# Two moves in the second layer: heads' products in turns on the two column halves, and slots and gathers of units 1 and 2 ahead of the experts' order

## The chip, the core and the metric

One core of a Trainium2 chip runs the whole program in one launch. The metric is the device time of an execution in microseconds; lower is better. TensorE (PE in the profile), VectorE (DVE), ScalarE (ACT), GpSimd (POOL) and the DMA queue of SyncE (SP) each work through their own list of instructions in order.

## The reference

A backbone of two layers over 256 latent tokens and 256 context tokens of width 1024, all in float32. Only the second (odd) layer is touched by the change. Cut to what matters:

```python
# odd mixer, latent tokens only (last layer)
y = concat([pool_branch(u_pool), latent_attention(q, k, v, k_c, v_c, sink)]) @ w_out
h = h + m[2] * y
f = modulate(rmsnorm(h, norm_ffn_g), m[3], m[4])
# latent_attention, per block of 128 queries and head: 8 heads of 64, 2 key/value heads
p = softmax(concat([s_lat, s_ctx, sink]))       # 256 latent + 256 context keys
o = p_lat @ v + p_ctx @ v_ctx
# grouped_moe: 16 experts, top 2 of one group of 4
out = sum_e combine[:, e] * ((silu(f @ w_gate[e]) * (f @ w_up[e])) @ w_down[e])
h = rmsnorm(h + m[5] * out)
```

## The kernel before

Everything in the second layer works on two chunks of 128 tokens. A tile framework schedules the written program: it orders the instructions of each engine by a timing model of its own, so a change in one place moves instructions around it.

**Weights** come as tiles of 1 MB (128 x 2048 floats) from one stream in a fixed order (`Stream`, line 100). `load` (L134 on) issues a tile's DMA on SP as soon as one of 13 places is free; `take`, `half` and `done` hand them to the matrix products and free them. Experts that are alone in a unit have each tile split into a high and a low part first (`_prep`: ACT makes `whi` at L176, DVE or POOL makes `wlo` at L180), and a product is then three products (`mm3`, L516, whose records are L517 to L519). An odd_w_out tile is treated the same way. Modulation weights (`ada`, L445) are multiplied as they are, in four strips of 32 columns of TensorE.

**Attention.** Eight units (`units`: a block of 128 queries b, a pair of heads c). `scores(b, c)` makes both heads' scores (L1498), the softmax on DVE and ACT (L1502 to L1518) and leaves `p` with 2 x 512 probabilities per query. `attend(b, c)` transposes p of one head in four pieces (L1530), copies them to `pTT` (L1532; DVE for the first head, ACT for the second) and multiplies the values by it in four products that add up (L1535). The first head's products write partitions 0 to 63 of the bank, the second's 64 to 127, so each uses one half of TensorE's columns. Between the units stand the pool branch (L1478, L1484), modulation weights (L445) and products with odd_w_out (`mix`).

**Experts.** The 16 experts stand in units of one (S), two (P) or four (Q): "PPSPSPPQ". A unit with n experts gives each 128/n of 128 slots. The first five experts, thus units 0, 1 and 2, are fixed; the others are put in order of load by `order` (from L984), whose result also chooses which expert's weights SP loads from there on (`ids`, a load into a register at L301). `arrange` (L1010) turns the token ranks into that order. `slots1(n)` finds with DVE compares (L1646) and TensorE products (L1650) which token sits in each slot; `gather1(n)` fetches these rows by an indirect DMA from POOL (L1664); `xpose1(n)` transposes them (L1679). For unit 0 `xpose1` gets the tokens by products with the slot matrix (L1682) and needs no gather. The loop over units then takes the up product, hidden, the transposition of the next unit, and its gate product (`gu`, records L933), with the down products (`down1`, L967) of the unit before. The gathered tile `xg` shares its two buffers with `f0` and `f1`, the layer's normed tokens, and `sgm` has two buffers.

Of the kernel before, what the change touches and what calls it, by code (L numbers as in the profile page):

```python
# [10 lines left out]
F32 = mybir.dt.float32  # L11
# [15 lines left out]
FIXED = (2, 5)  # L27
# [185 lines left out]
def backbone(ctx: ExitStack, tc: tile.TileContext, I, out):  # L213
    nc = tc.nc
    V, S, G, T, Q = nc.vector, nc.scalar, nc.gpsimd, nc.tensor, nc.sync
# [14 lines left out]
    def y_t():  # L230
        return psum.tile([128, 512], F32, name="yp", tag="yp", bufs=2)

    def tr_t():
        return psum.tile([128, 512], F32, name="tr", tag="tr", bufs=2)
# [107 lines left out]
    for half in range(2):  # L342
        v = owo[512:1024, half * 512:half * 512 + 512].rearrange("(j c d) n -> j d c n", j=2, c=4)
# [177 lines left out]
    def split(hi, lo, x, eng):  # L521
        i = S.activation(hi, x, AF.Copy)  # L522
        eng.tensor_sub(lo, x, hi.bitcast(F32))  # L523
        return i
# [117 lines left out]
    with phase("even") as ep:  # L642
# [78 lines left out]
        def banks4():  # L721
            return [mm_t() for _ in range(4)]
# [22 lines left out]
        b = banks4()  # L745
# [5 lines left out]
        b = banks4()  # L751
# [6 lines left out]
        b = banks4()  # L758
# [7 lines left out]
        b = banks4()  # L766
# [114 lines left out]
        for half in range(2):  # L881
            banks = [mm_t() for _ in range(4)]
            hs = slice(half * 512, half * 512 + 512)
# [102 lines left out]
    def order(l, pool, nch, oh):  # L986

        pk = tr_t()
        for c in range(nch):
            T.matmul(pk[0:16, 0:16], one[:, 0:16], oh[:, c], start=(c == 0), stop=(c == nch - 1))  # L990
        t16 = lambda n, name: pool.tile([16, n], F32, name=name, tag=name)
        key, kd, kc, place, over, cap = t16(16, "key"), t16(16, "kd"), t16(1, "kc"), t16(1, "place"), t16(1, "over"), t16(1, "cap")
        V.scalar_tensor_tensor(key, pk[0:16, 0:16], 32.0, kb[l], op0=OP.mult, op1=OP.add)
        V.tensor_mul(kd, key, idt[0:16, 0:16])
        V.tensor_reduce(kc, kd, axis=AX.X, op=OP.add)
        V.tensor_scalar(kd, key, kc, None, op0=OP.is_ge)
        V.tensor_reduce(place, kd, axis=AX.X, op=OP.add)
        perm = t16(16, "perm")
        V.tensor_scalar(perm, ior[0:16, 0:16], place, None, op0=OP.is_equal)
        pt = tr_t()  # L1000
        T.matmul(pt[0:1, 0:16], eid[0:16], perm, start=True, stop=True)
        V.tensor_copy(ids[l], pt[0:1, 0:16])
        V.tensor_mul(kd, perm, caps[l])
        V.tensor_reduce(cap, kd, axis=AX.X, op=OP.add)
        V.tensor_scalar(over, kc, kbe[l], 1.0 / 32, op0=OP.subtract, op1=OP.mult)
        V.tensor_sub(over, over, cap)
        return perm, cap, over
# [126 lines left out]
    with phase("moe0") as mp:  # L1134
# [17 lines left out]
        def id_weights(name, cw, n):  # L1152

            t = mp.tile([128, 4, n, 4], F32R, name=name)
            for j in (0, 3):
                V.tensor_copy(t[:, :, :, j], idk[:, :, None].to_broadcast([128, 4, n]))
            V.tensor_copy(t[:, :, :, 1], cw[:, :, 0:n])
            V.tensor_sub(t[:, :, :, 2], cw[:, :, 0:n], t[:, :, :, 1].bitcast(F32))
            return t

        ranks, idw = pm, id_weights("idw2", comb, 2)
        units = UNITS[0]
# [166 lines left out]
        for c in range(2):  # L1329
            t = ("whi", "wlo")[c]  # L1330
# [19 lines left out]
    with phase("odd") as op:  # L1350
# [14 lines left out]
        vv = op.tile([128, 4, 128], F32, name="vv")  # L1365
# [91 lines left out]
        for b in range(2):  # L1457
            pt = tr_t()
# [6 lines left out]
        pt = tr_t()  # L1465
# [55 lines left out]
        ob = {}  # L1521

        def attend(b, c):
            p = PN.pop((b, c))
            if c == 0:
                ob[b] = y_t()
            for v in range(2):
                pt = tr_t()
                for q in range(4):
                    T.transpose(pt[:, q * 128:(q + 1) * 128], p[:, v, q * 128:(q + 1) * 128], idt)  # L1530
                pT = op.tile([128, 4, 128], F32, name="pTT", tag="pTT", bufs=2)
                (S.copy if v else V.tensor_copy)(pT.rearrange("p k t -> p (k t)"), pt)  # L1532
                hs = slice(v * 64, v * 64 + 64)
                for q in range(4):
                    T.matmul(ob[b][hs, c * 128:(c + 1) * 128], vv[:, q, hs], pT[:, q], start=(q == 0), stop=(q == 3),  # L1535
                             skip_group_check=True)
            if c == 3:
                bs = slice(b * 128, b * 128 + 128)
                split(mT[1][0][:, :, bs], mT[1][1][:, :, bs], ob[b].rearrange("p (c t) -> p c t", c=4), V)

        units = [(b, c) for b in range(2) for c in range(4)]
# [32 lines left out]
        for n, u in enumerate(units):  # L1574
            if n + 1 < len(units):
                scores(*units[n + 1])
            if n < 4:
                f = pool_group(n)
            attend(*u)
            if n < 4:  # L1580
                f()
            if n < 6 - NPRE:
                ada(*next(ada_it))
            if n == 4:
                flush()
                rows(1, 3, 5, 1)
                t = op.tile([128, 2, D], F32, name="s4b", tag="band")
# [32 lines left out]
    with phase("moe1") as mp:  # L1620
# [5 lines left out]
        units = UNITS[1]  # L1626
# [12 lines left out]
        def slots1(n):  # L1639

            u = units[n]
            w = 128 // len(u)
            sg = mp.tile([128, 2, 128], F32, name="sgm", tag="sgm", bufs=2)
            for c in range(2):
                for h, p in enumerate(u):
                    V.tensor_scalar(sg[:, c, h * w:h * w + w], ior[:, 0:w], ranks[:, c, p:p + 1], None, op0=OP.is_equal)  # L1646
            pw_ = tr_t()
            m = 2 * len(u)
            for c in range(2):
                T.matmul(pw_[:, 0:m], sg[:, c], idw[:, c, u[0]:u[0] + len(u)].rearrange("p e j -> p (e j)"),  # L1650
                         start=(c == 0), stop=(c == 1))
            for h in range(len(u)):
                hs = slice(h * w, h * w + w)
                V.tensor_scalar(sli[hs, n:n + 1], pw_[hs, 2 * h + 1:2 * h + 2], OFF, None, op0=OP.add)
            t = mp.tile([128, 1], F32, name="slw1", tag="slw1", bufs=4)
            for h in range(len(u)):
                hs = slice(h * w, h * w + w)
                V.tensor_copy(t[hs], pw_[hs, 2 * h:2 * h + 1])
            slw[n] = t
            return sg  # L1660

        def gather1(n):
            xg[n] = cp.tile([128, D], F32, name=f"xg{n}", tag="H1", bufs=2)
            return G.indirect_dma_start(out=xg[n], out_offset=None, in_=fd1,  # L1664
                                        in_offset=bass.IndirectOffsetOnAxis(ap=sli[:, n:n + 1], axis=0),
                                        bounds_check=255, oob_is_err=False)

        def xpose1(n, sg=None):

            xh = mp.tile([128, KD, 128], F32R, name="xh1", tag="xh", bufs=2)  # L1670
            xl = mp.tile([128, KD, 128], F32R, name="xl1", tag="xl", bufs=1) if len(units[n]) == 1 else None
            for hf in range(2):
                pt = tr_t()
                for q in range(4):

                    ks = slice(hf * 4 + q, D, 8)
                    o = pt[:, q * 128:(q + 1) * 128]
                    if sg is None:
                        T.transpose(o, xg[n][:, ks], idt)  # L1679
                    else:  # L1680
                        for c in range(2):
                            T.matmul(o, f1[c][:, ks], sg[:, c], start=(c == 0), stop=(c == 1))  # L1682
                fs = slice(hf * 4, hf * 4 + 4)
                if xl is None:
                    (V.tensor_copy if hf else S.copy)(xh[:, fs].bitcast(F32).rearrange("p k t -> p (k t)"), pt)
                else:
                    split(xh[:, fs], xl[:, fs], pt.rearrange("p (k t) -> p k t", k=4), V)
            xT[n] = (xh, xl)
# [23 lines left out]
        st.more(1, lambda: Two(x_t("wa", "X"), x_t("wb", "X")))  # L1712
        st.load()
        idw = id_weights(comb)
        xpose1(0, slots1(0))
        perm, cap, over = order(1, mp, 2, oh)
        st.limit = st.upto = 1 << 30
        st.load()
# [1 line left out]
        pg = gu("g", 1, 0, *xT[0])  # L1720
        ranks, combS, ranksT = arrange(1, mp, 2, perm, pm, comb, "amt")
        idw = id_weights(combS)
        for n in (1, 2):
            slots1(n)
            gather1(n)
        reg = any_over(mp, over)
# [29 lines left out]
        for half in range(2):  # L1756
            hs = slice(half * 512, half * 512 + 512)
# [107 lines left out]
```

## Time and profile before

| | |
|---|---|
| median of 3 runs (lowest, highest) | 1009.97 us (1009.04, 1010.44) |
| the profiled execution's own time | 1012.91 us |
| its span, first to last instruction | 1011.1 us |
| mean granted TensorE clock | 0.958 of full |
| busy: PE, DVE, ACT, POOL | 92%, 53%, 34%, 34% |
| DMA moved | 296.28 MB, mean 293 GB/s |

An fp32 product leaves two records on PE, a transposition one: "x8" at L1535 is four products. PE's busy time is modelled and neighbours overlap by some 0.07 us, so the length of a group is best read from its start to the next group's start. A bracket at a row's end tells how long the engine stood idle before it, and for what.

### The profile page before, as it was taken

To read this page: it belongs to the slowest core of one execution; us is meant where nothing else is said; L and a number is where in the kernel's file an instruction comes from. 1 tells how busy PE (TensorE), PEld (TensorE's weight loads), DVE (VectorE), ACT (ScalarE), POOL (GpSimd) and SP (SyncE) were. 2 spreads that over 40 slices of the span, in tenths; PEclk is the share of its full clock that TensorE was granted. 3 is DMA by queue.
4 is the path that set the end of the run, shared out by engine and by line. 5 is a ranking of instruction groups with operands and counts; after the bars stand their busy time and mean duration, and the time that the engine had idled before them with its cause. 6 is when DMAs were issued, how large, how long until landed. Compare 5 with 4: busy or idle time off the path is not lost. (4 is left out here: it accounts for less than half of the span.)

```text
span 1011.1 us, 12687 instructions
## 1 busy us (share of the span) xinstructions
PE 927.9 (92%) x4662; PEld 583.7 (58%) x4662; DVE 532.2 (53%) x921; ACT 340.3 (34%) x488; POOL 346.5 (34%) x239
## 2 busy tenths in 40 slices
PE   4999999978899999999999788999976999999973
PEld 2677677746675678558746567457553355544321
DVE  4552525286783777457935774547443265643212
ACT  4322113144563266246534362333211132411001
POOL 3350103335562746525823633023000143452112
PEclk9999999998899999999999989799977999999988
DMA  9973668948699799799699872296568799999993
GB/s 316 363 266 125 230 252 290 352 167 299 214 321 374 245 344 362 264 340 387 219 363 385 292 237 84 94 308 237 191 232 326 293 418 407 370 384 419 420 397 132
DMA packets 116276, 296.28 MB, mean 293 GB/s; under 512 B 6632, under 2 KB 16888, under 8 KB 105704
## 3 DMA queue, kind: packets, MB, share of 16 engines
q1 hardware_dynamic: 110184, 278.06, 75.0%
q0 software_dynamic: 5984, 17.26, 4.7%
q8 instruction: 40, 0.66, 0.3%
q14 instruction: 36, 0.29, 0.1%
q10 hardware_dynamic: 32, 0.01, 0.0%
HBM read 295.45 MB, written 4.24 MB: 296 GB/s over the span
## 5 line engine op out<-in xcount | busy, mean ns | idle before, releaser
L176 ACT ACTIVATE whi<-w 128x1024 fp32r<-128x1024 f32 x182 | 190.7, 1058 | 221.9 <-PE mm L519 87.0
L180 POOL TENSOR_TENSOR wlo<-w,whi 128x1024 fp32r<-128x1024 f32 x64 | 164.6, 2572 | 258.8 <-ACT whi L176 206.0
L180 DVE TENSOR_TENSOR wlo<-w,whi 128x1024 fp32r<-128x1024 f32 x118 | 181.1, 1546 | 92.5 <-ACT whi L176 91.8
L933 PE MATMUL mm<-w,xh 128*64 128x512 f32 (+1 forms) x616 | 150.9, 617 | 4.8 <-DMA w<-in_moe_w_up_dram 4.8
L528 POOL TENSOR_TENSOR H<-H,am 128x512 f32<-128x512 f32 x64 | 89.7, 1420 | 125.3 <-DVE am L527 122.9
L933 PEld LDWEIGHTS mm<-w,xh 128*64 128x64 f32 (+1 forms) x616 | 43.8, 135 | 88.4 <-issue 78.1
L517 PE MATMUL mm<-whi,xh 128*128 128x512 f32 x192 | 79.3, 413 | 1.9 <-DVE am L527 1.1
L518 PE MATMUL mm<-wlo,xh 128*128 128x512 f32 x192 | 78.6, 409 | 2.7 <-DVE wlo L180 2.3
L519 PE MATMUL mm<-whi,xl 128*128 128x512 f32 x192 | 78.1, 407 | 0.0
L527 DVE TENSOR_TENSOR am<-mm,m5b 128x512 f32<-128x512 f32 x64 | 42.9, 684 | 28.7 <-PE mm L1261 19.5
L1261 PE MATMUL mm<-y,seT 128*128 128x512 f32 x208 | 54.5, 397 | 0.2 <-ACT y L522 0.2
L517 PE MATMUL mm<-aTh,whi 128*128 128x512 f32 x128 | 52.4, 415 | 1.0 <-ACT aTh L678 1.0
L518 PE MATMUL mm<-aTl,whi 128*128 128x512 f32 x128 | 51.6, 403 | 1.1 <-POOL aTl L679 1.1
L519 PE MATMUL mm<-aTh,wlo 128*128 128x512 f32 x128 | 51.1, 400 | 0.0
L1261 PEld LDWEIGHTS mm<-y,seT 128*128 128x128 f32 x208 | 38.1, 188 | 15.5 <-issue 4.9
L518 PEld LDWEIGHTS mm<-wlo,xh 128*128 128x128 f32 x192 | 37.4, 195 | 14.4 <-DVE wlo L180 3.4
L517 PEld LDWEIGHTS mm<-whi,xh 128*128 128x128 f32 x192 | 37.5, 195 | 14.0 <-issue 4.2
L445 PE MATMUL yp<-w,sT 128*32 128x512 f32 x288 | 44.0, 624 | 0.0
L519 PEld LDWEIGHTS mm<-whi,xl 128*128 128x128 f32 x192 | 37.4, 195 | 7.7 <-DVE xl L523 0.3
L517 PE MATMUL yp<-whi,hh 128*128 128x512 f32 x96 | 38.2, 397 | 0.7 <-ACT hh L1067 0.7
L1053 DVE SCALAR_TENSOR_TENSOR sg<-sg,slw,mm 128x512 f32<-128x512 f32 x21 | 15.6, 742 | 43.9 <-PE mm L933 41.1
L518 PE MATMUL yp<-wlo,hh 128*128 128x512 f32 x96 | 38.4, 400 | 0.0
(363 smaller groups left out, 1545.2 us busy)
## 6 DMA issues: line engine op xcount, KB each, us to landing
w<-in_moe_w_gate_dram SPq DMA_DIRECT2D x60, 1024.0 KB, 11.3
w<-in_moe_w_down_dram SPq DMA_DIRECT2D x59, 1024.0 KB, 10.5
w<-in_moe_w_up_dram SPq DMA_DIRECT2D x57, 1024.0 KB, 9.7
w<-in_ada_w_dram SPq DMA_DIRECT2D x48, 1024.0 KB, 10.1
w<-in_even_w_in_dram SPq DMA_DIRECT2D x8, 1024.0 KB, 9.6
w<-in_odd_w_in_dram SPq DMA_DIRECT2D x5, 1024.0 KB, 14.3
w<-in_even_w_out_dram SPq DMA_DIRECT2D x4, 1024.0 KB, 7.9
s4b<-mrow SPq DMA_DIRECT2D x6, 512.0 KB
```

Source lines behind the costliest of these rows:

```text
L176: self.nc.scalar.activation(hi, t, AF.Copy)
L180: eng.tensor_sub(lo, t, hi.bitcast(F32))
L445: T.matmul(pa[32 * j:32 * j + 32, :], s_at(s * 4 + j, u), t[:, j, :], start=first and s == 0, stop=last and s == 1, skip_group_check=True)
L517: T.matmul(o, lh, rh, start=first, stop=False)
L518: T.matmul(o, lh, rl, start=False, stop=False)
L519: T.matmul(o, ll, rh, start=False, stop=last)
L527: V.tensor_mul(t, pp, m)
L528: eng.tensor_add(acc, acc, t)
L933: T.matmul(o[hs], xh[:, kk, hs].bitcast(F32), w[h][:, k], start=first and k == 0, stop=last and k == 3, skip_group_check=True)
L1053: V.scalar_tensor_tensor(sg, sg, w, pu, op0=OP.mult, op1=OP.mult)
L1261: marks["comb"] = T.matmul(pp, seT[n][:, c * 128:(c + 1) * 128], t[:, hs], start=(i == 0), stop=(i == 2 * len(ns) - 1))
```

## The change

In `attend`, both heads' pieces are now transposed and copied first, and the eight products then go in turns: piece 0 of the first head, piece 0 of the second, piece 1 of the first, and so on. In the experts' stage, `slots1(1)` now stands between `slots1(0)` and `xpose1(0)`, `gather1(1)` behind `xpose1(0)`, then `slots1(2)` and `gather1(2)`, all ahead of `order`; they use the ranks from before the sorting, which are the same for fixed experts. The same two calls behind `arrange` are gone. Lines behind the first edit are numbered three higher in the changed kernel, and those behind the second eleven higher.

```diff
             if c == 0:
                 ob[b] = y_t()
+            pT = []
             for v in range(2):
                 pt = tr_t()
                 for q in range(4):
                     T.transpose(pt[:, q * 128:(q + 1) * 128], p[:, v, q * 128:(q + 1) * 128], idt)
-                pT = op.tile([128, 4, 128], F32, name="pTT", tag="pTT", bufs=2)
-                (S.copy if v else V.tensor_copy)(pT.rearrange("p k t -> p (k t)"), pt)
-                hs = slice(v * 64, v * 64 + 64)
-                for q in range(4):
-                    T.matmul(ob[b][hs, c * 128:(c + 1) * 128], vv[:, q, hs], pT[:, q], start=(q == 0), stop=(q == 3),
+                pT.append(op.tile([128, 4, 128], F32, name="pTT", tag="pTT", bufs=2))
+                (S.copy if v else V.tensor_copy)(pT[v].rearrange("p k t -> p (k t)"), pt)
+
+            for q in range(4):
+                for v in range(2):
+                    hs = slice(v * 64, v * 64 + 64)
+                    T.matmul(ob[b][hs, c * 128:(c + 1) * 128], vv[:, q, hs], pT[v][:, q], start=(q == 0), stop=(q == 3),
                              skip_group_check=True)
...
         idw = id_weights(comb)
-        xpose1(0, slots1(0))
+
+        ahead = [n for n in (1, 2) if units[n][-1] < FIXED[1]]
+        sg0 = slots1(0)
+        slots1(1)
+        xpose1(0, sg0)
+        gather1(1)
+        for n in ahead[1:]:
+            slots1(n)
+            gather1(n)
         perm, cap, over = order(1, mp, 2, oh)
...
-        for n in (1, 2):
+        for n in range(1 + len(ahead), 3):
             slots1(n)
             gather1(n)
```

**PE, units 0 and 1 of attention.** (tr is a bank for transpositions, yp one for sums, sT the conditioning columns.) Before:

```order
L1530 MATMUL tr<-idt,p 128x128 x8
L1535 MATMUL yp<-pTT,vv 64x128 x4
L1484 MATMUL tr<-pT,pw 128x256
L445 MATMUL yp<-w,sT 32x512 x5
L1535 MATMUL yp<-pTT,vv 64x128 x4
L445 MATMUL yp<-w,sT 32x512 x3
L1478 MATMUL tr<-band,U 128x256 x2
L445 MATMUL yp<-w,sT 32x512 x5
L1530 MATMUL tr<-idt,p 128x128 x4
L445 MATMUL yp<-w,sT 32x512 x11
```

Now:

```order
L1531 MATMUL tr<-idt,p 128x128 x8
L1538 MATMUL yp<-pTT,vv 64x128
L1484 MATMUL tr<-pT,pw 128x256
L445 MATMUL yp<-w,sT 32x512 x9
L1538 MATMUL yp<-pTT,vv 64x128 x7
L1478 MATMUL tr<-band,U 128x256 x2
L1531 MATMUL tr<-idt,p 128x128 x4
L445 MATMUL yp<-w,sT 32x512 x15
L1498 MATMUL mm<-kT,qT 128x512 x2
```

The first product of a unit goes alone where the first four went, and the other seven stand where the second four stood. The modulation products (L445) between them stand in groups of 9 and 15 instead of 5, 3, 5 and 11. Over all eight units the L445 groups counted in products are 5, 3, 5, 11, 5, 1, 2 and 4, 1, 11 before, and 9, 15, 8 and 11, 5 now. The products of the last two units stand as one group of eight, those of the other six as one and seven. Scores (L1498) behind unit 0's products stand four times alone and twice as a pair before, twice alone and three times as a pair now.

**PE, from the end of unit 0's up products to the gate products of unit 1.** (xh is the transposed input, idw the slots' token numbers and weights.) Before:

```order
L933 MATMUL mm<-w,xh_6447 64x512 x11
L1019 MATMUL tr<-perm,pmT 128x16 x2
L1024 MATMUL tr<-idt,comb 16x128 x2
L1029 MATMUL tr<-perm,cbT 128x16 x2
L1033 MATMUL tr<-pmT,perm 16x256
L1650 MATMUL tr<-idw_6540,sgm 128x4 x2
L1650 MATMUL tr<-idw_6540,sgm 128x2 x2
L1074 MATMUL tr<-idt,over 1x16
L1046 MATMUL tr<-pmST,idt 64x256 x2
L1679 MATMUL tr<-idt,xg_6556 128x128 x8
L1650 MATMUL tr<-idw_6540,sgm 128x4 x2
L933 MATMUL mm<-w,xh_6646 64x512 x21
```

Now:

```order
L933 MATMUL mm<-w,xh_6460 64x512 x3
L1019 MATMUL tr<-perm,pmT 128x16 x2
L1024 MATMUL tr<-idt,comb 16x128 x2
L1029 MATMUL tr<-perm,cbT 128x16 x2
L1033 MATMUL tr<-pmT,perm 16x256
L1074 MATMUL tr<-idt,over 1x16
L1046 MATMUL tr<-pmST,idt 64x256 x2
L1682 MATMUL tr<-idt,xg_6481 128x128 x8
L1653 MATMUL tr<-idw_6570,sgm 128x4 x2
L933 MATMUL mm<-w,xh_6646 64x512 x21
```

The four products of `slots1` for units 1 and 2 (two rows of x2) no longer stand between L1033 and L1074. They went ahead of unit 0's gate products: two between L592 and the first of `xpose1(0)`, two behind its last. The product of `order` (L990) moved from ahead of the 16 gate products of unit 0 to behind 13 of them, and L1001, which gives `ids`, from behind 16 products L933 to behind 29.

**SP, behind the loads of `ids` and of the overflow flag.** One piece of the difference:

```order
-L147 DMA w<-in_moe_w_gate_dram 128x2048
-L147 DMA w<-in_moe_w_down_dram 128x2048 x4
-L147 DMA w<-in_moe_w_up_dram 128x2048
...
+L147 DMA w<-in_moe_w_down_dram 128x2048 x2
+L147 DMA w<-in_moe_w_gate_dram 128x2048
+L147 DMA w<-in_moe_w_down_dram 128x2048
+L147 DMA w<-in_moe_w_up_dram 128x2048
+L147 DMA w<-in_moe_w_down_dram 128x2048
```

Before, the second half of unit 2's gate weights leads and the four tiles of unit 1's down weights follow it; now two of these go first. The register loads of `ids` also stand together behind unit 2's first gate tile, all but one.

## Rows read from the trace of the kernel before

**Rows 1.** Windows of the trace: PE, PEld, DVE, ACT, POOL busy; clock, DMA share, GB/s.

```profile
653.00:725.00 72.00, 71.28 (x433) 42.18 (x432) 40.93 (x88) 27.52 (x61) 17.00 (x13) 1.00 0.79 262
...
741.00:784.00 43.00, 33.96 (x151) 19.90 (x153) 13.60 (x59) 4.94 (x6) 2.16 (x2) 0.78 0.80 315
784.00:800.00 16.00, 16.00 (x68) 5.47 (x64) 4.46 (x9) 2.60 (x3) 3.36 (x2) 0.93 0.61 225
800.00:991.00 191.00, 177.66 (x839) 83.72 (x838) 77.23 (x116) 37.98 (x51) 58.37 (x39) 0.97 1.00 403
```

**Rows 2.** Timeline of PE, attention: start, length (us), engine, line, records.

```profile
650.63 1.97 PE L1535 MATMUL yp<-pTT,vv 128*64 128x128 f32 x8
...
653.44 1.90 PE L445 MATMUL yp<-w,sT 128*32 128x512 f32 x10
655.28 1.09 PE L1535 MATMUL yp<-pTT,vv 128*64 128x128 f32 x8
656.29 1.06 PE L445 MATMUL yp<-w,sT 128*32 128x512 f32 x6
...
660.77 2.78 PE L445 MATMUL yp<-w,sT 128*32 128x512 f32 x22
663.47 1.12 PE L1498 MATMUL mm<-kT,qT 64*128 64x512 f32 x2
...
673.68 1.13 PE L1498 MATMUL mm<-kT,qT 64*128 64x512 f32 x4
...
723.11 1.71 PE L1535 MATMUL yp<-pTT,vv 128*64 128x128 f32 x16
725.50 0.50 PE L517 MATMUL mm<-whi,mh 128*128 128x512 f32 x1 [0.69 <-ACT mh L522]
```

**Rows 3.** Timeline of PE, three groups elsewhere that use part of the columns or few.

```profile
690.71 1.06 PE L481 MATMUL tr<-csm,part 128*128 128x8 f32 x8
...
720.46 0.43 PE L635 MATMUL tr<-hT,rws 128*32 128x128 f32 x8
...
823.29 7.32 PE L967 MATMUL yp<-w,hh 128*64 128x512 f32 x32
```

**Rows 4.** Timeline of ACT in the attention.

```profile
668.29 2.00 ACT L176 ACTIVATE whi<-w 128x1024 fp32r<-128x1024 f32 x2 [2.43 <-DMA w<-in_odd_w_out_dram]
```

**Rows 5.** A window of 10 us late in the attention (columns as in rows 1).

```profile
690.00:700.00 10.00, 10.00 (x70) 7.51 (x68) 8.95 (x22) 3.96 (x10) 3.77 (x3) 1.00 0.33 111
```

**Rows 6.** Timeline of PE, from unit 0's slots to unit 1's gate products.

```profile
742.68 0.56 PE L1650 MATMUL tr<-idw,sgm 128*128 128x4 f32 x2 [0.83 <-DVE sgm L1646]
...
767.82 0.61 PE L1019 MATMUL tr<-perm,pmT 16*128 16x16 f32 x4
...
771.09 1.02 PE L1650 MATMUL tr<-idw,sgm 128*128 128x4 f32 x8 [0.69 <-DVE idw L1635]
...
773.56 1.12 PE L1046 MATMUL tr<-pmST,idt 16*64 16x256 f32 x4 [0.86 <-DVE ovs L1076]
780.14 1.94 PE L1679 MATMUL tr<-idt,xg 128*128 128x128 f32 x8 [5.46 <-DMA xg<-fd,sli]
...
783.31 11.10 PE L933 MATMUL mm<-w,xh 128*64 128x512 f32 x42
```

**Rows 7.** Timeline of DVE in the same stretch.

```profile
742.12 0.74 DVE L1646 TENSOR_SCALAR sgm<-cst,posm 128x64 f32<-128x64 f32 x4
...
770.43 0.41 DVE L1035 CAST pmST<-tr 16x256 fp32r<-16x256 f32 x1
...
773.41 0.57 DVE L1646 TENSOR_SCALAR sgm<-cst,pmS 128x128 f32<-128x128 f32 x2
```

**Rows 8.** Timeline of POOL, unit 1's gather.

```profile
772.83 1.13 POOL L1664 DMA_INDIRECT xg<-fd,sli  x1 [33.67 <-PE tr L1074]
```

**Rows 9.** Timeline of SP's queue, unit 2's gate and unit 1's down weights.

```profile
768.19 15.46 SPq L147 DMA_DIRECT2D w<-in_moe_w_gate_dram  x2
793.14 2.05 SPq L147 DMA_DIRECT2D w<-in_moe_w_down_dram  x4
```

## The prediction

> **What bounds the kernel now.** I read the windows first. In the attention, 653 to 725 us, PE is busy 71.28 of 72 us at full clock, DVE 40.93, ACT 27.52, DMA 0.79 [rows 1]: PE is the bound there, and its timeline says on what. Between 741 and 784, the head of the experts' stage, PE is busy 33.96 of 43 us at clock 0.78, so something is waited for. From 800 to 991 DMA stands at 1.00 and 403 GB/s, with PE at 177.66 of 191: the weights stream without a break and the end of the kernel hangs on them. The places that DMA fills are freed by PE, so a microsecond that PE gains ahead of 800 lets the whole stream run a microsecond earlier. Just ahead, 784 to 800, DMA is at 0.61: it starves, for want of places or behind a wait on its queue. So the question for each part is how much earlier PE and SP reach that stream.
>
> **The products of the heads.** One head's four products (eight records) take 1.01 us, start to start (655.28 to 656.29), sixteen in a row 1.71 [rows 2]: 0.107 a record and 0.16 for each group. A head uses 64 of TensorE's 128 columns, and that is paid in full now. What two halves in turns bring is shown by the down products: 32 records of 512 moving columns in 7.32 us, 0.23 each [rows 3], where a lone score product of two records, also of 512, takes 1.12, about 0.45 a record after the entry [rows 2]. So two run at once. The sixteen records of a unit then cost 8 x 0.107 + 0.16 = 1.02. Six units stand as one and seven: the lone one 0.38 (two records), the seven 1.02 (an odd one and three pairs make four rounds), 1.40 against 2.02, 0.62 saved each, 3.7 in all. The last two stand as eight: 1.02 against 2.02 and 1.71, 1.7 saved. Sum 5.4.
>
> Could each record be held at 0.107 by its weight load, with nothing to share? Eight records with only 8 moving columns but 128 weight columns take 1.06, that is 0.11 to 0.13 each, so loads do set a floor; but eight with 32 weight columns and 128 moving take 0.43 [rows 3], under 0.054 each. For 64 columns I take half of the 128's, about 0.06, against 0.053 that turns want: 0.1 a unit at worst, neglected.
>
> **What moves with them.** Modulation products use four strips of 32 columns: groups of 3, 5 and 11 products (6, 10 and 22 records) take 0.99, 1.84 and 2.70 [rows 2], so a round of up to four costs 0.85 and a group 0.14. The order lists give 17 rounds in ten groups before, 14 in five now: 3 x 0.85 + 5 x 0.14 = 3.2 saved. A score product costs 1.12 alone and two together 1.13 [rows 2]; six such turns become five: 1.1 saved. Transpositions, copies and DMAs of this part keep their number, and the copies (0.7 each) lie beside PE's work.
>
> Sum 9.7. Against it stand new waits. A unit's products now need both copies. ACT's second pair of odd_w_out conversions waits for its landing until 668.29 and holds ACT to 670.3 [rows 4]; adding up the new order from 650.63 (modulation 8.1, heads' products 2.9, scores 2.1, pool and transpositions, by an estimate, 5.9) I reach the first products with odd_w_out at 669.7, and the low part of pool group 1, copied by ACT behind that pair, is wanted at 670.9 but there only near 671.5. With a few such joints I deduct 1.5: **8.2 us** earlier at 725.50, where `mix` of the second chunk begins. From there to the slots of unit 0 nothing changes.
>
> **Slots and gathers.** Removed: from the end of unit 0's products (767.82) to the transposition of unit 1 (780.14) PE spends 12.3 us, of which 5.46 is the wait for the gather, issued on POOL only at 772.83, and 0.69 + 1.02 stand for the slot products [rows 6, 8]. Now the gather can go once `xpose1(0)` has read `f0`, near 752, some 20 us ahead of need, against 7.3 from issue to use. What is left behind 767.82 is `arrange` to its cast at 770.43 + 0.41 [rows 7], then L1074 and L1046 (1.12), so unit 1's transposition can begin 4.4 us after 767.82: 7.9 saved. Added ahead of unit 0's gate products: two slot products more at the slow clock (about 0.5 [rows 6]), part of four more compares (0.74 [rows 7]), and behind `xpose1(0)` the compares for unit 2 (0.57 [rows 7]), which wait for the slot buffer that `xpose1(0)` reads, then two more slot products (0.5). I take 1.9. POOL has nothing behind the two gathers but later splits, and SP is not asked. Net on PE **6.0 us** at unit 1's gate products (783.31 [rows 6]).
>
> SP's queue gains more. Before, unit 2's second gate tile leaves only at 783.65 (768.19 + 15.46), and unit 1's down tiles stand behind it until 793.14 [rows 9], since the first of them wants the place that this gate tile holds until it is split. Now two down tiles stand ahead of it and want only unit 1's first gate products, some 4 us behind 777.3. DMA would run from about 781.5 instead of 793.1, less the 2.5 us of the one tile that went in between: 9 us ahead. `order` now gives `ids` (L1001) three products of 0.5 us ahead of the end of unit 0's up products, near 767.82 + 1.9 - 1.5 = 768.2, 13 products (6.5 us) later than before; SP reads it for tiles that want the last of these products anyway, so it is covered. If that cover were gone, 6.5 us would come off this part.
>
> The stream thus starts between 6.0 (PE frees places) and 9 (SP) earlier; since PE is nearly full through it too, I stay near the first: **6.6**. Total 14.8. The profiled execution would take 1012.91 - 14.8 = 998.1; it lies 2.94 above the median 1009.97, so the prediction is **995.2**.
>
> **Rivals.** (B) *No sharing.* The products stay bound by weight loads at 0.107 a record: 5.4 falls away, 1000.6. For it: 1.06 for eight records with hardly anything to move [rows 3]. Against it: 0.43 with narrow weights and 0.23 for the down products [rows 3]. The Trainium skill, "TensorE: Matmul & The Clock Gate", Part 3 (What overlaps and what doesn't), says that a weight load overlaps with running products only when their row groups differ. Both heads use all 128 rows, so by that rule the time would be B's 1000.6; the down products use all rows too, and the trace disagrees there with 0.23 us a record. 10%.
>
> (C) *The softmax chain.* Late in the attention DVE is busy 8.95 of 10 us [rows 5]. If it can't be pressed further, what PE saves behind 690 (some 3 us) goes into waits for `p`: first part 5, total 11.6, 998.4. Against it: the stage of 690 to 710 shrinks little in the new order, most is saved ahead of it. 13%.
>
> (D) *The head doesn't pass on.* If the landing of unit 2's gate tiles still sets when the stream starts, only the first part is left: 8.2, 1001.8. For it: 15.46 us for two tiles [rows 9]. Against it: the two down tiles that go ahead. 12%. With B as well, 2.8 is left: 1007.2, 2%.
>
> (E) *Slower.* If waits for the second head's copy break PE's work between 656 and 716 so often that TensorE falls to 1.2 of its 2.4 GHz, every group there doubles: eight records took 1.97 at 650.63, when it was low, and 1.09 at 655.28 [rows 2]. That decides once more than 14.8 us of work in this stretch runs at the low level; with 20 us of it the time is 995.2 + 20 = 1015.2. Against it: the clock is 1.00 from 653 to 725 [rows 1], and the new order puts modulation, pool or score products between a unit's first product and the other seven. 3%.
>
> **How the numbers follow.** Forecast 58%, with a range of its own of 991.5 to 998.5 (first part 6 to 9.7, second 5.5 to 9); B 10%, C 13%, D 12%, B with D 2%, the edits cancelling to nothing 2%, E 3%. 0.2% (2 us) is about what a measurement of this kernel can tell from no change. B, C and D lie over 2 us below 1009.97, so faster 0.95, same 0.02, slower 0.03. The range 990.5 to 1003.5 takes in the forecast's own bounds, B, C and D with 2 us around the outermost, and leaves out B with D, nothing and E.
>
> **What would show it.** Right: sixteen product records of a unit in two groups of about 0.4 and 1.0; `mix` of the second chunk near 717; no wait for xg at unit 1's transposition; its gate products some 14 us ahead of 783.31; down tiles of unit 1 leaving within 5 us of these; DMA at 1.00 from about 773 to 976. Wrong: groups of seven at 1.5 or more (B); PE idle on `p` or pTT with DVE near full (C); a hole in DMA behind unit 2's gate tile as long as before (D); a clock under 1.00 between 650 and 715 (E).

## The result and the profile after

In the first comparison the changed kernel took 1001.09 us (median of 4 runs, 999.21 to 1002.79) against 1010.21 us; a second one gave 999.51 against 1011.66. The ratios are 0.9879 (95% interval 0.9837 to 0.9922) and 0.9881 (0.9856 to 0.9906): some 12 us faster where 14.8 were forecast. They are not the quotients of these medians: the first pair lies only 9.1 us apart (0.9910, inside the interval), the second 12.2. The time lies inside the range, but 4 to 6 us above the forecast of 995.2 and outside the 991.5 to 998.5 of the forecast itself. By the time alone it could as well be rival B (1000.6) or D (1001.8), so the trace has to decide. The profiled execution of the change took 1002.48 us (span 1000.6), against 1012.91 (1011.1) before.

Windows of the changed kernel, set where those of [rows 1] stand in its own course (columns as there):

```profile
653.00:717.00 64.00, 61.48 (x425) 36.50 (x423) 40.59 (x92) 27.04 (x60) 17.78 (x13) 0.99 0.84 270
733.00:773.00 40.00, 36.39 (x161) 20.93 (x163) 14.48 (x79) 3.05 (x4) 3.12 (x3) 0.80 0.88 343
773.00:790.00 17.00, 17.00 (x77) 5.76 (x76) 6.10 (x6) 4.61 (x5) 2.36 (x1) 0.99 0.93 361
790.00:981.00 191.00, 176.73 (x824) 81.93 (x820) 84.22 (x116) 37.78 (x53) 57.36 (x40) 0.97 0.98 392
```

The attention is shorter, and the head of the experts' stage no longer stands idle: PE is busy 36.4 of 40 us there, before 34.0 of 43, and the DMA share just ahead of the stream is 0.93 instead of 0.61. But the stream itself now runs at 0.98 and 392 GB/s, where it had 1.00 and 403 [rows 1]; the prediction asked for 1.00 from about 773 on.

PE's timeline in the attention, answering to [rows 2]:

```profile
656.36 1.09 PE L1538 MATMUL yp<-pTT,vv 128*64 128x128 f32 x14
...
658.88 3.63 PE L445 MATMUL yp<-w,sT 128*32 128x512 f32 x30
...
675.26 0.43 PE L1538 MATMUL yp<-pTT,vv 128*64 128x128 f32 x2 [0.31 <-DVE pTT L1533]
677.11 1.09 PE L1538 MATMUL yp<-pTT,vv 128*64 128x128 f32 x14 [0.79 <-ACT pTT L1533]
...
712.41 1.09 PE L1538 MATMUL yp<-pTT,vv 128*64 128x128 f32 x16
...
719.06 0.50 PE L517 MATMUL mm<-whi,mh 128*128 128x512 f32 x1 [0.69 <-ACT mh L522]
```

Fourteen and sixteen records now take what eight took before, 1.09 as the row models it. Modulation stands in five groups (the largest of 30 records) instead of ten. The two waits for a copy of `pTT` are new, as is a third of 0.19 at 717.29.

PE's timeline in the head, answering to [rows 6], and the rows of POOL and SP that answer to [rows 8] and [rows 9]:

```profile
736.77 1.84 PE L1653 MATMUL tr<-idw,sgm 128*128 128x4 f32 x8 [0.83 <-DVE sgm L1649]
...
746.76 6.22 PE L933 MATMUL mm<-w,xh 128*64 128x512 f32 x26
...
766.09 1.77 PE L1682 MATMUL tr<-idt,xg 128*128 128x128 f32 x8
...
768.47 12.12 PE L933 MATMUL mm<-w,xh 128*64 128x512 f32 x42
...
787.07 0.64 PE L967 MATMUL yp<-wa,hh 128*64 128x512 f32 x1
...
746.31 1.09 POOL L1667 DMA_INDIRECT xg<-fd,sli  x1 [14.29 <-PE tr L1685]
...
774.61 0.81 SPq L147 DMA_DIRECT2D w<-in_moe_w_down_dram  x2
```

The 5.46 us that unit 1's transposition waited for its gather are gone: that gather now leaves POOL at 746.31, 20 us ahead of need. On SP's queue unit 1's first down tiles leave at 774.61, against 793.14 [rows 9].

**Where the time went.** The runs of one program differ by some us already ahead of the attention, where nothing was changed. So I read stretches between four places that every version has: (A) the eight score products that follow a wait of 1.6 us for `p`, ahead of the first products of heads (row 644.36 of the kernel before); (B) `mix` of the second chunk; (D) the first of unit 0's down products; (E) the end of the span. Of each kernel one execution was profiled, of the kernel before and of the change two:

| us | A to B | B to D | D to E | A to E |
|---|---|---|---|---|
| before | 81.1 | 75.4 | 210.2 | 366.7 |
| before, second profile | 80.7 | 76.7 | 210.3 | 367.7 |
| the change | 73.7 | 68.0 | 213.5 | 355.3 |
| the change, second profile | 73.9 | 67.8 | 212.9 | 354.6 |

By the means 7.1 us are won in the attention and 8.2 in the head, together 15.3, and 3.0 are given back behind the first down product: 12.3 in all. The two profiles of a kernel agree within 0.6 us from D on, so the loss belongs to the change. Ahead of D the scatter is larger: over all profiles of this document A to B is 80.7 to 81.2 without turns and 72.7 to 75.3 with them.

### The profile page after: what moved, and what is told of

It reads as the page before. It is cut to its first block, busy times and chain, and to the rows that moved or that the text cites. A ratio compares the mean times of both kernels' runs of the same rounds, so it can differ in the third digit from the quotient of the medians.

```text
span 1000.6 us, 12686 instructions
## 1 busy us (share of the span) xinstructions
PE 920.2 (92%) x4662; PEld 577.3 (58%) x4662; DVE 537.9 (54%) x921; ACT 339.3 (34%) x488; POOL 345.1 (34%) x239
## 5 line engine op out<-in xcount | busy, mean ns | idle before, releaser
L180 DVE TENSOR_TENSOR wlo<-w,whi 128x1024 fp32r<-128x1024 f32 x118 | 186.2, 1590 | 91.3 <-ACT whi L176 90.7
L933 PE MATMUL mm<-w,xh 128*64 128x512 f32 (+1 forms) x616 | 152.2, 616 | 4.6 <-DMA w<-in_moe_w_up_dram 4.6
L933 PEld LDWEIGHTS mm<-w,xh 128*64 128x64 f32 (+1 forms) x616 | 42.5, 135 | 89.0 <-issue 77.7
L519 PE MATMUL mm<-whi,xl 128*128 128x512 f32 x192 | 77.6, 404 | 0.0
L445 PE MATMUL yp<-w,sT 128*32 128x512 f32 x288 | 41.0, 627 | 0.0
L519 PE MATMUL yp<-whi,hl 128*128 128x512 f32 x96 | 37.8, 401 | 2.0 <-DVE hl L1068 2.0
```

Source lines behind the costliest of these rows:

```text
L180: eng.tensor_sub(lo, t, hi.bitcast(F32))
L445: T.matmul(pa[32 * j:32 * j + 32, :], s_at(s * 4 + j, u), t[:, j, :], start=first and s == 0, stop=last and s == 1, skip_group_check=True)
L519: T.matmul(o, ll, rh, start=False, stop=last)
L933: T.matmul(o[hs], xh[:, kk, hs].bitcast(F32), w[h][:, k], start=first and k == 0, stop=last and k == 3, skip_group_check=True)
```

## The experiments

**The two parts, each alone.** `e1` is the change without its edit in the head, so the kernel before with products in turns alone:

```diff
-        ahead = [n for n in (1, 2) if units[n][-1] < FIXED[1]]
-        sg0 = slots1(0)
-        slots1(1)
-        xpose1(0, sg0)
...
+        xpose1(0, slots1(0))
```

`e2` is the change without its edit in the attention:

```diff
-            for q in range(4):
-                for v in range(2):
-                    hs = slice(v * 64, v * 64 + 64)
...
+                hs = slice(v * 64, v * 64 + 64)
+                for q in range(4):
...
```

> The kernel before with the heads' products in turns alone; slots and gathers stay behind the experts' order. Theory (both parts pass on to the end, each by what it gains at its own place): the mix of the second chunk comes 6.4 to 7.4 us earlier than in the kernel before, as in the profile of the change, and the end with it: about 1010.2 - 7 = 1003. Rival 1 (the stream's start is set by unit 2's gate tile behind the gather, not by PE): the gain at the mix stays, the end moves by under 2 us: 1008 to 1010. Rival 2 (all of the gain comes from here, the head's part gives nothing): 1001, as the whole change.

> The kernel before with slots and gathers of units 1 and 2 ahead of the order alone; products head by head. Theory: unit 1's gate products come about 8.4 us earlier than in the kernel before (783.31 there), as they do in the change relative to the mix, and the end with them unless the VectorE split of 8.3 us near 875 shows here too: 1010.2 - 8 = 1002 without it, about 1006 with it. Rival (the head's gain is eaten by the stream, which is full to the end): the gate products are 8 us earlier, the end under 2: 1008 to 1010.

`e1` took 1007.00 us, 0.9943 of the kernel before (0.9925 to 0.9961); `e2` 1004.52, 0.9912 (0.9883 to 0.9942). The kernel before took 1012.72 there, not 1010.2, so all expectations are read as differences: 5.8 and 8.9 us less, where the theory had 7 and 8, and together 14.7, close to the 14.8 of the forecast. The whole change has less, some 12, though the intervals overlap. The stretches of their single profiles say where: `e1` wins 8.2 from A to B and gives 1.5 back from B to D (77.6) and 1 from D to E (211.2); `e2` wins 8.5 from B to D and gives nothing back (209.7). Both parts reach the end for the most part, against the rivals that leave one of them under 2 us, and only the two together have the long tail (`e8_add3V` and `e5_unit1` below have it too: 212.4 and 214.1). The split of 8.3 us shows in neither.

**Turns, or only a new grouping?** In `e3_noturn` both heads are still transposed and copied first, but the products run head by head:

```diff
-            for q in range(4):
-                for v in range(2):
+            for v in range(2):
+                for q in range(4):
```

> The whole change, both heads' probabilities transposed and copied first as there, but the products head by head instead of in turns. Theory (two column halves run side by side): sixteen records in a row take 1.7 us again where the change has 1.02, fourteen 1.5 or more; the six units and the last two lose up to 5.4 us, the end comes about 4 to 5 us later than that of the change: 1005 to 1006. Rival (the first part's gain came from the new grouping of modulation and score products, not from turns): products as long as in the change or the end within 1.5 us of it: 1000 to 1002.5.

Its PE timeline:

```profile
652.25 1.09 PE L1538 MATMUL yp<-pTT,vv 128*64 128x128 f32 x8
...
664.98 1.09 PE L1538 MATMUL yp<-pTT,vv 128*64 128x128 f32 x8
...
720.08 1.72 PE L1538 MATMUL yp<-pTT,vv 128*64 128x128 f32 x16
...
722.49 0.51 PE L517 MATMUL mm<-whi,mh 128*128 128x512 f32 x1 [0.69 <-ACT mh L522]
```

Eight records take 1.09 again and sixteen 1.72, though the weights, the data and the number of records are the same: within a unit only the order of the halves differs. A to B is 80.7 us, so 6.9 of the 7.1 are lost, more than the 5.4 that products alone account for: the modulation groups are ten again. The order of a unit's products also decides how the scheduler packs the modulation between them, so the sum's second term was a consequence of the first. At the end, however, `e3_noturn` took 1002.63, 0.9907 (0.9873 to 0.9942), only some 3 us more than the change, between the 4 to 5 of the theory and the 1.5 of the rival, and the intervals overlap: its D to E is 210.1. In this pair, by A to E of the profiles (357.9), under half of the attention's 7 us reach the end.

**What the tail lost.** DVE, POOL and SP's queue around the large hole in the DMA of the changed kernel:

```profile
871.90 2.52 POOL L528 TENSOR_TENSOR H<-H,am 128x512 f32<-128x512 f32 x2 [10.95 <-DVE am L527]
...
875.51 8.30 DVE L180 TENSOR_TENSOR wlo<-w,whi 128x1024 fp32r<-128x1024 f32 x1
875.59 2.51 POOL L528 TENSOR_TENSOR H<-H,am 128x512 f32<-128x512 f32 x2
878.05 2.36 POOL L180 TENSOR_TENSOR wlo<-w,whi 128x1024 fp32r<-128x1024 f32 x1
880.38 2.35 POOL L180 TENSOR_TENSOR wlo<-wb,whi 128x1024 fp32r<-128x1024 f32 x1
883.73 1.21 DVE L180 TENSOR_TENSOR wlo<-wa,whi 128x1024 fp32r<-128x1024 f32 x1
883.93 0.33 SPq L147 DMA_DIRECT2D w<-in_moe_w_gate_dram  x1
```

One low-part subtraction of a weight split takes 8.30 us on DVE, the next one 1.21. It begins with POOL's additions and ends about one undisturbed length behind POOL's last subtraction, which ends at 882.73. SP's gate load, which needs the place that this split frees, leaves right behind it, and DMA runs dry. In windows of the change:

```profile
875.00:880.00 5.00, 5.00 (x26) 1.77 (x24) 5.00 (x2) 1.54 (x2) 4.98 (x4) 1.00 0.91 369
880.00:885.00 5.00, 3.57 (x16) 1.27 (x12) 5.00 (x3) 0.60 (x1) 2.72 (x2) 1.00 0.10 20
```

Share 0.10 for 5 us is 4.5 us of the stream. In the second profile the same split takes 8.28 at 873.62. In the kernel before, POOL's additions and splits of that unit are spread from 886.19 to 899.0. `e4_engV` takes all splits of this stage off POOL, one line in `moe1`:

```diff
         ranks, ranksT = pm, None
+        st.eng = V
```

> The whole change, with every low-part subtraction of a weight split in the second experts' stage on VectorE, none on GpSimd (every third stood there). Theory (the 4 us between the gain at the down products of unit 0 and the gain at the end were lost where VectorE's split took 8.3 us at 875.5 beside three GpSimd operations, which held the queue's next gate load back): no split there over 2.5 us, the hole in the DMA at 880 to 890 (share 0.51) is gone, and the end comes about 4 us earlier: 996 to 998. Rival 1 (the hole comes from the places of the stream or a landing): it stays, 1000 to 1003. Rival 2 (VectorE is too full for the additional subtractions of 1.2 us): later than 1003, with PE waiting for wlo.

It took 993.35 us (991.90 to 995.75), 0.9804 (0.9776 to 0.9832): it beats both kernels, and by more than I expected. Its timeline and its windows at the same place:

```profile
873.44 2.50 POOL L528 TENSOR_TENSOR H<-H,am 128x512 f32<-128x512 f32 x2
...
875.83 2.35 DVE L180 TENSOR_TENSOR wlo<-w,whi 128x1024 fp32r<-128x1024 f32 x2
878.09 1.22 DVE L180 TENSOR_TENSOR wlo<-wa,whi 128x1024 fp32r<-128x1024 f32 x1
878.21 0.33 SPq L147 DMA_DIRECT2D w<-in_moe_w_gate_dram  x1
```

```profile
875.00:880.00 5.00, 5.00 (x23) 1.99 (x20) 4.57 (x5) 0.60 (x1) 0.93 (x1) 1.00 0.84 306
880.00:885.00 5.00, 5.00 (x20) 3.23 (x19) 0.45 (x1) 0.00 (x0) 0.00 (x0) 1.00 0.96 354
```

Two splits take 2.35, the gate load leaves 7.1 us earlier (counted from D: 89.7 us behind it, in the change 96.9), and the hole is gone. D to E is 205.4, 7.8 less than the mean of the change's two.

A hole stands there without the long split too. In `e3_noturn` no split on DVE takes over 3.4 us, and the same gate load stands behind a subtraction on POOL, itself at 3.33 instead of 2.36:

```profile
879.70 3.33 POOL L180 TENSOR_TENSOR wlo<-w,whi 128x1024 fp32r<-128x1024 f32 x1
...
883.06 0.33 SPq L147 DMA_DIRECT2D w<-in_moe_w_gate_dram  x1
```

```profile
879.00:884.00 5.00, 4.02 (x18) 1.65 (x15) 1.81 (x1) 0.60 (x1) 5.00 (x3) 1.00 0.19 75
```

The load leaves 93.5 us behind D, in `e2` too, 3.3 earlier than in the change, and D to E is 210.1 and 209.7, so 3.1 and 3.5 shorter. In all fourteen profiles the end comes 115.7 to 119.0 us behind this load, while the load itself leaves between 85.3 (`e7_beforeV`, below) and 97.9 (`e5_unit1`) behind D: the tail follows it. `e4_engV` takes away two things at once, the collisions and the slower subtractions on POOL (2.36 against 1.21); no run parts them.

**Is that the loss of the change?** The saving is larger than the loss, so the same edit was put into the kernel before and into each part alone:

> The kernel before with every weight split's subtraction of the second experts' stage on VectorE, none on GpSimd: the edit that took the whole change to 993.35 (e4_engV). Theory (the change moved two GpSimd splits behind two additions and so made a new stall in the tail, which the kernel before hardly has): it gains only what the old stall at 814.76 (5.62 us for one split) costs, 2 to 4 us: 1008 to 1011 beside 1012.7 for the kernel before there. Rival (GpSimd's splits cost the tail as much in both kernels, so the change lost nothing to them): 6 to 8 us less, about 1005 to 1006.

> Products in turns alone (as e1), with all splits of the second experts' stage on VectorE. Theory (without GpSimd's splits in the way the two parts pass on to the end in full): 7 us less than the kernel before with the same splits (e7_beforeV). Rival (the stream sets the end, part of the gain is lost even so): under 4 us less than it.

> Slots and gathers ahead alone (as e2), with all splits of the second experts' stage on VectorE. Theory: 8 us less than the kernel before with the same splits (e7_beforeV), and 7 more than the whole change with them (993.35, 0.9804 of the kernel before). Rival (the two parts share one gain): within 3 us of the whole change with them.

| splits on DVE | median, us | ratio to before (95%) | A to B | B to D | D to E | A to E |
|---|---|---|---|---|---|---|
| before (`e7_beforeV`) | 1005.51 | 0.9930 (0.9914 to 0.9945) | 81.1 | 77.3 | 203.0 | 361.4 |
| turns alone (`e1V`) | 1000.07 | 0.9894 (0.9877 to 0.9912) | 74.4 | 77.1 | 202.7 | 354.1 |
| head alone (`e2V`) | 998.18 | 0.9857 (0.9826 to 0.9888) | 80.9 | 67.7 | 206.1 | 354.7 |
| whole (`e4_engV`) | 993.35 | 0.9804 (0.9776 to 0.9832) | 74.1 | 68.0 | 205.4 | 347.5 |

My theory expected 1008 to 1011 for `e7_beforeV`; the rival's 1005 to 1006 came. POOL's splits cost the kernel before about as much (D to E falls by 7.3 there, by 7.8 in the change), without a stall of 8 us: the longest splits on DVE behind D take 5.62, 4.21 for two in a row, 2.07, 1.70 and 1.64. The kernel before took 1012.78 beside these runs (1012.72 beside `e4_engV`). The change's own effect with splits on DVE is 0.9804 / 0.9930 = 0.987, the same as with them on POOL, or 13.8 us against 12.3 from A to E. So the stall is real and worth removing, but against the kernel before, which has stalls of its own, it explains little of the missing 2.5 us: between nothing (by the ratios, which leave some 3 us either way) and 1.5 us (by single profiles, of which only 0.6 lie behind D).

What the rest is, the windows from D to E tell. Of the kernel before and of the change:

```profile
800.89:1011.10 210.21, 183.68 (x868) 85.23 (x866) 81.69 (x124) 42.02 (x60) 63.51 (x44) 0.96 0.92 371
```

```profile
787.07:1000.60 213.53, 185.58 (x868) 84.56 (x866) 90.98 (x125) 42.09 (x62) 64.20 (x45) 0.96 0.90 362
```

and with splits on DVE, before (`e7_beforeV`) and whole (`e4_engV`):

```profile
804.73:1007.70 202.97, 180.99 (x868) 83.29 (x866) 85.22 (x131) 41.77 (x60) 47.80 (x37) 0.96 0.93 378
```

```profile
788.48:993.90 205.42, 181.40 (x868) 82.89 (x866) 85.60 (x133) 42.62 (x62) 46.25 (x37) 0.97 0.93 378
```

With splits on POOL the change has no more left to move at D than before (213.53 x 362 = 77.3 MB, before 210.21 x 371 = 78.0, and 77.4 in its second profile), but moves it more slowly: holes. With splits on DVE the rate is the same, 378, but the whole change has 0.9 MB more to move (77.6 against 76.7), and 0.9 MB at 378 GB/s are 2.5 us: PE arrives at D 16 us earlier, but the weights have not come forward as far. One pair alone would say little, since the two profiles of the kernel before differ by 0.6 MB; but `e1V`, without the head's edit, has 76.0 MB left at D, and `e2V` and `e9_allV` (below), with it, 77.5 each, with D to E of 202.7 against 206.1 both times. So a few us of what PE wins ahead of D do not reach the end, which hangs on weights moved. `e1V` and `e2V` divide it, by single profiles: turns reach the end in full (7.2 us from A to E, of 6.7 won from A to B), the head with 6.7 of 9.6. The times don't confirm this for turns: `e1V` is 5.4 us below `e7_beforeV` by the medians and 3.6 by the ratios, so between the theory's 7 and the rival's 4, or within the rival. That turns pass on in full is not shown. `e2V` is 7.3 below `e7_beforeV`, where the theory had 8, and 4.8 above the whole, where it had 7.

**Moving only the colliding additions.** `e8_add3V` gives the four additions of unit 3's combination to DVE:

```diff
-                    add_mod(am, H[c][:, hs], pp, m5b[:, hs], G)
+                    add_mod(am, H[c][:, hs], pp, m5b[:, hs], V if n == 3 else G)
```

> The whole change with four additions moved alone: those of unit 3's combination, the ones that stand on GpSimd at 871.9 and 875.59 in the change, go to VectorE. Theory (the split of 8.30 us at 875.51 stood still for the GpSimd operations of 875.59 to 882.73, and the queue's next gate load, 883.93, with it): the split takes under 3.7 us, the gate load leaves some 4 to 6 us earlier, the DMA share of 880 to 885 (0.10) is above 0.5, and the end comes about 3 to 4 us earlier than in the change: 0.983 to 0.985 of the kernel before. Rival (the hole comes from something else, and the whole edit of e4_engV was needed): 0.987 to 0.99 and the hole stays.

```profile
876.91 2.37 POOL L180 TENSOR_TENSOR wlo<-w,whi 128x1024 fp32r<-128x1024 f32 x1
877.06 5.68 DVE L528 TENSOR_TENSOR H<-H,am 128x512 f32<-128x512 f32 x2
879.22 2.36 POOL L180 TENSOR_TENSOR wlo<-wb,whi 128x1024 fp32r<-128x1024 f32 x1
...
882.67 1.21 DVE L180 TENSOR_TENSOR wlo<-w,whi 128x1024 fp32r<-128x1024 f32 x1
...
884.00 0.33 SPq L147 DMA_DIRECT2D w<-in_moe_w_gate_dram  x1
```

The split takes 1.21 as the theory asked, but the gate load leaves at 884.00, the hole stays (0.09 from 880 to 885), and the time is 999.81, 0.9873 (0.9854 to 0.9891): no gain. The collision only changed its victim. Two additions on DVE, 0.68 each a little earlier, now take 5.68 beside POOL's two splits, and the split waits behind them. So it is no matter of one instruction: a split and an addition, both with two inputs in SBUF, stand still alike while POOL works through a row of tile operations.

`e9_allV` therefore leaves POOL none of the units' work but the gathers (the edit of `e4_engV`, and the additions of every unit):

```diff
+        st.eng = V
...
-                    add_mod(am, H[c][:, hs], pp, m5b[:, hs], G)
+                    add_mod(am, H[c][:, hs], pp, m5b[:, hs], V)
```

> The whole change with both kinds of GpSimd arithmetic of the second experts' stage on VectorE: the splits' subtractions (as in e4_engV) and the additions of the combinations. Theory (a VectorE operation with two inputs in SBUF stands still while GpSimd adds or subtracts tiles; nothing is left to collide): no split and no addition on VectorE over 2.5 us behind unit 0, and at least the time of e4_engV: 992 to 994 beside about 1012.8 before, 0.980. Rival (VectorE becomes the bound, with some 32 additions of 0.7 us more): PE waits for wlo or hl, 996 or later.

It took 995.19 us, 0.9837 (0.9814 to 0.9860), between the theory's 992 to 994 and the rival's 996: nothing better than `e4_engV`, from A to E 348.1 against 347.5. No split and no addition on DVE is stretched any longer, but that gains nothing more than splits on DVE alone; SP's queue waits for splits, not for additions.

**Unit 1 alone ahead.** `e5_unit1` leaves unit 2 behind the order:

```diff
-        ahead = [n for n in (1, 2) if units[n][-1] < FIXED[1]]
+        ahead = [1]
```

> The change with slots and gather of unit 1 alone ahead of the experts' order; those of unit 2 behind it as before. Theory (the head's gain is the gather of unit 1; unit 2's is not waited for): gate products of unit 1 as early as in the change or 0.5 to 1 us earlier, the end within 2 us of it. Rival (unit 2's gather goes into a wait of its own at its transposition): later by 3 us or more.

It took 1005.24 us, 0.9929 (0.9901 to 0.9957), 2 us (A to E: 356.9) to 5 us more than the change (by the ratios, whose intervals just overlap); I had expected none beyond 2. Its PE timeline behind unit 0's products:

```profile
767.94 0.58 PE L1653 MATMUL tr<-idw,sgm 128*128 128x2 f32 x4 [0.69 <-DVE idw L1638]
...
768.92 1.12 PE L1046 MATMUL tr<-pmST,idt 16*64 16x256 f32 x4 [0.31 <-DVE ovs L1076]
769.97 1.97 PE L1682 MATMUL tr<-idt,xg 128*128 128x128 f32 x8
```

Unit 2's gather is not waited for (no bracket ahead of its transposition either, 797.26). What costs is that its slot products stand between unit 0's products and unit 1's again, with their wait for `idw`: B to unit 1's gate products is 51.9 us there, 49.4 and 50.0 in the change; D to E is the longest of all, 214.1.

**Repeats.** The second profiles of the table above:

> The whole change again, on the chip of these runs, for a second profile of it. If the 3.3 us that the stretch from unit 0's down products to the end is longer than before (213.5 against 210.2) belong to the change, it is again 212.5 to 214.5; if they were one execution's accident, within 1 us of 210.2. Time: 0.988 of the kernel before by the theory that nothing depends on the chip.

> The kernel before again, for a second profile of it: the stretch from unit 0's down products to the end 210.2 to within 1 us, if that stretch repeats; the stretch ahead of the attention may differ by some us, as it did from 641.75 to 646.55 between runs whose code there is the same.

Both came as expected: 212.9 and 210.3 from D to E, 0.9881 and 0.9999 of the kernel before.

## Why the prediction was right, and where not

- *Turns run two halves at once*: right. Sixteen records take 1.09 where head by head they take 1.72. Rival B falls. With it falls the time that followed there from the rule of the Trainium skill ("TensorE: Matmul & The Clock Gate", Part 3, What overlaps and what doesn't): both heads use all rows, and the sixteen records still take 1.09. The prediction's 0.107 a record and 0.16 a group don't give the 1.71 that they were read from (16 x 0.107 + 0.16 = 1.87), but the 1.02 that was worked out with them came.
- *5.4 + 3.2 + 1.1 less 1.5 for waits, 8.2 at the mix*: 7.1 (73.7 and 73.9 us from A to B, against 81.1 and 80.7). By the starts of the rows the products gain 5.8, modulation 2.9 and scores 1.1, so the 9.7 came. The waits are larger: 0.79, 0.31 and 0.19 for the copies, and 0.88 ahead of the first products with odd_w_out, by the profile until ACT had made `p`, not for the low part that the prediction had named; 2.2 in all, and 2.7 in the second profile, where that one is 1.43. These 0.7 to 1.2 more are most of the 1.1 that lacks.
- *6.0 in the head at unit 1's gate products*: 8.0 (B to these 57.8 and 57.6 before, 49.4 and 50.0 after). Added work was well sized (1.7 of the 1.9 from the mix to unit 0's gate products); what was removed is larger, 3.6 us from the end of unit 0's products to unit 1's transposition, where I had left 4.4, and this stretch now runs at a higher clock: the granted clock from B to D is 0.85 and 0.87, before 0.82.
- *The head's 6.6 as taken at the end*: with splits on DVE it is 6.6 to 6.7 (`e2V` against `e7_beforeV`, `e4_engV` against `e1V`, A to E of single profiles), less than PE's gain, as the bound by the stream would have it. There the number was right, with splits elsewhere than in the change.
- *"so a microsecond that PE gains ahead of 800 lets the whole stream run a microsecond earlier"*: this is the step that failed. PE was 15.3 us earlier at D, more than the 14.2 that the sum has for PE (8.2 + 6.0), and 12.3 came out. The stream lost some 3 us behind D, to a stall of 8.3 us on DVE that holds SP's queue, and, where POOL's splits are removed from both kernels, 2.4 us, to weights that have not come forward as far as PE. The sentence *"POOL has nothing behind the two gathers but later splits"* saw the splits but not what stands on DVE beside them. That the total came within 3 us is in part luck: 2.0 more in the head stand against 1.1 less at the mix and 3.0 lost in the tail.
- *The range*: its ends lie 1.0 and 1.7 us outside of 991.5 and 1001.8, not 2 as said; nothing hangs on it.
- Rivals C and D did not come: PE waits for no `p` behind 690, and SP's down tiles leave 18.5 us earlier, though 6.1 us behind unit 1's gate products and not within 5. E neither: the clock is 0.99 from 653 to 717.

Open is how much of the 3 us the one stall at 875 costs by itself: on the change, what was tried either moved it (`e8_add3V`) or removed all of its kind (`e4_engV`). `e2` and `e3_noturn`, which lack it and whose gate load leaves 3.3 us earlier, come nearest with a D to E some 3 us shorter, but other splits differ there as well. Open too is why the two parts together, but neither alone, pack POOL's work so, and how much of the turns' gain reaches the end: 3 to 7 us by the pairs above.

## What to carry to other kernels

Time that a leading stage wins reaches the end only as far as the stream that the end hangs on comes forward with it: count the bytes still to be moved at the joint, and look what holds the queue's loads behind it, not only at the engine's arrival there. Before work is shared between VectorE and GpSimd, look whether both read tiles from SBUF at the same time, above all where a queue waits for the result. Where column halves are free, order products so that neighbours use different halves; the scheduler may then pack other work better as well.

## What was not expected of the hardware

A VectorE operation with both inputs in SBUF stood through a whole row of GpSimd operations, not through one: 8.30 and 8.28 us in the two profiles of the change, beside additions and two subtractions without a gap, where it takes 1.21 alone; in `e8_add3V` two additions of 0.68 each took 5.68. POOL waits as well: in `e3_noturn` a subtraction took 3.33 beside a split on DVE, where it takes 2.36 else. In the change, rows 75 to 80 us earlier show the contrast:

```profile
796.88 2.57 POOL L528 TENSOR_TENSOR H<-H,am 128x512 f32<-128x512 f32 x2 [7.27 <-DVE am L527]
797.32 0.68 DVE L527 TENSOR_TENSOR am<-mm,m5b 128x512 f32<-128x512 f32 x1
...
800.63 2.55 POOL L528 TENSOR_TENSOR H<-H,am 128x512 f32<-128x512 f32 x2
800.94 5.65 DVE L180 TENSOR_TENSOR wlo<-w,whi 128x1024 fp32r<-128x1024 f32 x1
803.13 2.37 POOL L180 TENSOR_TENSOR wlo<-w,whi 128x1024 fp32r<-128x1024 f32 x1
```

With one input in PSUM (`mm`) the operation keeps its 0.68 beside POOL; with two in SBUF it takes 5.65. The Trainium skill, "SBUF — State Buffer", Who interferes with whom, says that a VectorE instruction with two SBUF inputs contends with a GpSimd instruction that reads SBUF, and that the later one blocks until the first has finished. The trace agrees on which operations collide; on the length it shows more, since the wait lasted for all the GpSimd operations of the row, not for one instruction.
